# An encoder trunk step on one core: reloads of activations at the stage changes issued from POOL's queue instead of SP's

## The chip, the core and the metric

The kernel runs on one core of a Trainium2 chip, as one launch. The time is in device microseconds of that core; the smallest of the shown runs is 1948.55 us, the largest 1949.81 us. The kernel's instructions are placed by a framework that works out the waits and the order on each engine when the kernel is built: engines are PE (TensorE, matmuls), ACT (ScalarE), DVE (VectorE), POOL (GpSimd) and SP (SyncE, which here only issues DMAs).

## The reference, cut to what matters

One inference step over 512 prompt frames and 32 frames of a running stream, 544 columns in all, with a model width of 2048. There are two layers and a final norm:

```python
def rec_layer(...):                                  # layer 0
    proj = rms_norm(x, g) @ w_in
    xa, ga, xb, gb = jnp.split(proj, ...)
    ya, h_new = rg_lru(causal_conv(xa, ...), ...)    # recurrence over the frames
    yb, pool_new = pool_mix(xb, ...)                 # trailing means over 2/4/8/16 frames
    mixed = jnp.concatenate([ya * silu(ga), yb * silu(gb)], axis=-1)    # 3072 wide
    return x + mixed @ w_out, ...

def att_layer_prompt(x, g, w_in, w_out):             # layer 1
    q, k, v, gt = att_inputs(x, g, w_in)             # rms_norm(x, g) @ w_in, 16 heads of 128
    o = ...                                          # stick-breaking attention, 128-query blocks
    return x + (o * silu(gt)) @ w_out, k, v

y = rms_norm(x, norm_final)
```

All of it is in float32, and the outputs are y, k, v and the new states of the recurrent layer.

## The kernel before, in words

**Products.** Activations lie transposed, 128 features on the partitions and 544 frames along a row, so a 2048-wide activation is 16 such rows and the 3072-wide `mixed` is 24. A float32 product is made of three matmuls of a shorter type: each operand is split into a high part (a rounded copy, ACT) and the rest (a subtraction, DVE), and `mm3` (L108, L109, L110) multiplies high by high, low of x by high of w, and high of x by low of w. Weights come in pieces of 128 x 768 through `raw` (L195, on SP's queue, into seven buffers `wraw`) and are split by `wsplit` (L203 on ACT, L204 on DVE, into three pairs `wh`, `wl`); a `wraw` buffer is free when L204 has read it. PE runs without a loop, one output block after another.

**Blocks.** Twelve rows of an activation form a 2 x 2 block matrix, of two groups of six rows and two halves of 272 frames; the four quarters are called B11, B12, B21, B22. A `unit` multiplies two output blocks at once with a scheme of seven block products in place of eight; it needs the quarters and four sums and differences of them (T1 to T4) in split form. These forms lie in seven slots (`XH`, `XL`), where T4 has the slot of B12. A `plain_unit` needs only the quarters. Rows past the twelve are kept whole and split (`XP`, the names `xp`), and `rest` multiplies them.

**Stage changes.** An activation that one stage writes (`mixd`, `x2g` and `ogd` are such tensors in DRAM, as is `xgd` in the first layer) is read back, since the next stage needs it in block form. The stores go through `store` and `flush` (L326, SP's queue). The reads go through three functions, which the change touches:

- `fetch` (L233, its DMA at L237) loads one third of a quarter, two rows of 272 frames (128 x 2 x 272, 272 KB). `quarters` loads all four quarters, twelve DMAs, while the last unit of the stage before is still running, as its slots come free. `sums_by_pairs` loads quarters again for the sums T1 to T3: three DMAs for each of three pairs, then two subtractions and an addition on DVE (L283, L284, L285) and the splits (L230 on ACT, L231 on DVE); then three more loads for T4.
- `mixed_rows` (L776, its DMA at L780) loads rows 12 to 23 of `mixd`, a row of 128 x 544 (272 KB) with each DMA.
- `rows` (L1033, its DMA at L1037) loads rows 12 to 15 of `x2g` or `ogd` in the same way.

There are 92 such loads: 12 of `xgd`, in the first layer, for the sums alone, and three stage changes. The first change goes from the first layer's input product to its output product: quarters of `mixd` in the last unit, then the twelve rows, which `plain_unit` uses one after another, then the sums, 36 loads. The second goes from the first layer's output to head 0 of the second layer: quarters of `x2g` in the last unit, then four rows and the sums, 28 loads. The third goes from head 15 to the output product of the second layer: quarters of `ogd`, and much later its four rows, 16 loads.

**What sets the order.** Functions called hooks are run between the block products of a unit (the numbers in `quarters`, and the dictionaries given to `unit`); a load is written in the code one or two hooks ahead of its split. Each engine executes its own list in order, and the build's scheduler orders that list by its own estimates, so a load that stands on another queue can also move instructions of other engines. SP's list holds the weights' loads, the stores and, before the change, the 92 loads, some of them behind weight loads that wait for a `wraw` buffer. POOL's list holds a few copies, memsets and selects (for example L875 to L882, which build masks at the start of the second layer), and one DMA, the store of the last row of `mixd` (L766). A tile from the pool `tp` (`T()` in the code) takes a load's data: 8 buffers in the first layer's input product, 21 in its output product, 14 in the second layer.

**Around these.** Results leave PE's banks (`pp`, four of them) by evictions: on DVE L810 (with L809) in the first layer's output product, and L449 (with L447) in the attention's projection, where the result is also scaled by `rbc`. `L578` is a small POOL copy in the recurrent stage and `L694` a memset there.

Of the kernel before, what the change touches and what calls it, by code (L numbers as in the profile page):

```python
# [42 lines left out]
NS = 6  # L43
# [18 lines left out]
def trunk_step(ctx, tc, xT, w_in_rec, w_out_rec, gates, pool_w, vecs, st_h, st_conv, st_pool,  # L62
               w_in_att, w_out_att, ck, cv, y, kout, vout, hout, convout, poolout):
    nc = tc.nc
# [12 lines left out]
    def T(dt=F32, shape=(P, N)):  # L77
        return pools.tp.tile(list(shape), dt, tag="T", name=nm("T"))
# [146 lines left out]
    def fresh_row(j):  # L225
        XP.append(tuple(xs.tile([P, N], F32R, tag=f"xp{q}{j}", name=nm("xp")) for q in "hl"))
        return XP[-1]

    def xsplit(h, l, src):
        nc.scalar.activation(h, src, AF.Copy)  # L230
        nc.vector.tensor_tensor(l, src, f(h), ALU.subtract)  # L231

    def fetch(src, s, c):  # L233

        k, h = RAW[s]
        t = T(shape=(P, 2, HN))
        nc.sync.dma_start(t, src[:, k + 2 * c:k + 2 * c + 2, h])  # L237
        return t

    def made(s, c, t):  # L240
# [27 lines left out]
    def sums_by_pairs(src):  # L268
# [3 lines left out]
        def load(c):  # L272
            def fn():
                st[c] = [fetch(src, s, c) for s in (B12, B11, B22)]
            return fn
# [14 lines left out]
        def lastload():  # L290
            for c in range(NS // 2):
                st[c] = fetch(src, B21, c)
# [160 lines left out]
    mixd = dp.tile([P, 24, N], F32, tag="mixd", name="mixd")  # L453
    x2d = dp.tile([P, KT, N], F32, tag="x2d", name="x2d")
    x2g = dp.tile([P, KT, N], F32, tag="x2g", name="x2g")
    with ExitStack() as l0:
# [206 lines left out]
        for n in range(1, NRB):  # L663
            c = SimpleNamespace()
# [62 lines left out]
        for g4 in range(NPG):  # L727
            c = SimpleNamespace(ms=[])
# [43 lines left out]
    with ExitStack() as l0b:  # L772
# [3 lines left out]
        def mixed_rows(j0, j1):  # L776
            ts = []
            for j in range(j0, j1):
                t = T()
                nc.sync.dma_start(t, mixd[:, 2 * NS + j, :])  # L780
                ts.append(t)

            def fn():
                for j, t in zip(range(j0, j1), ts):
                    if j < 4:
                        hi, lo = fresh_row(j)
                    else:
                        hi, lo = T(F32R), T(F32R)
                        XP.append((hi, lo))
                    xsplit(hi, lo, t)  # L790
            pend.append(fn)
# [29 lines left out]
        for u in range(KT // 2):  # L821
            srcs = (w_out_rec[2 * u], w_out_rec[2 * u + 1])
            load, out = x2_out(u, SimpleNamespace())
            if u == 0:
                plain_unit(srcs, out, {
                    0: lambda: mixed_rows(0, 4),
                    1: lambda: (made_rows(), mixed_rows(4, 7)),
                    2: lambda: (made_rows(), mixed_rows(7, 10)),
                    3: lambda: (made_rows(), mixed_rows(10, 12)),
                    4: lambda: (made_rows(), load())})  # L830
            elif u == 1:
                plain_unit(srcs, out, {
                    0: loads[0],
                    1: lambda: (makes[0](), loads[1]()),
                    2: lambda: (makes[1](), loads[2]()),
                    3: lambda: makes[2](),
                    4: load, 5: lastload})
            else:
                hk = {2: load}
                if u == 2:  # L840
                    hk[0] = three
                last = u == KT // 2 - 1
                if last:
                    quarters(x2g, hk)
                unit(srcs, out, hk, LAST if last else ORDER)
# [4 lines left out]
    with ExitStack() as l1:  # L850
# [151 lines left out]
        def s_av(c):  # L1002
            w2, o_ps = c.w2, c.o
            mm3(o_ps, w2[:, 0, :P], w2[:, 1, :P], w2[:, 0, P:], w2[:, 1, P:], False, True)
            ob = e()[:, :P]
            for hh in range(4):
                rows = slice(hh * DEC, (hh + 1) * DEC)
                nc.vector.tensor_copy(ob[rows], o_ps[rows, hh * P:(hh + 1) * P])
            c.ob = ob
# [23 lines left out]
        def rows(src):  # L1033
            ts = []
            for j in range(4):
                t = T()
                nc.sync.dma_start(t, src[:, 2 * NS + j, :])  # L1037
                ts.append(t)

            def fn():  # L1040
                for j, t in enumerate(ts):
                    hi, lo = fresh_row(j)
                    xsplit(hi, lo, t)
            return fn
# [4 lines left out]
        for h in range(NH):  # L1049
            hh, G = h % 4, h // 4  # L1050
            c = SimpleNamespace()
            ha, hb = {}, {}
            if h == 0:
                rps = att_tile()
                box = []

                def spread_rbc():
                    with tc.high_priority():
                        nc.scalar.activation(rbc, rstd_spread(rps, box[0]), AF.Copy)
                with_hooks(ha, {0: [lambda: pend.append(rows(x2g))],  # L1060
                                1: [lambda: box.append(rstd_sums(rps, 0, N)), one, lambda: pend.pop()()],
                                2: [two], 3: [three],
                                4: [spread_rbc]})
            else:
                with_hooks(ha, {1: [lambda: (v_turn(prev), w_turn(prev))], 4: [lambda: av(h - 1, prev)]})
# [199 lines left out]
```

## Time and profile before

| what | value |
|---|---|
| time, median of 3 runs | 1948.99 us (1948.55 to 1949.81) |
| the profiled execution: time | 1951.53 us |
| the profiled execution: span | 1949.7 us |
| mean granted clock of TensorE | 0.994 of full speed |
| PE busy | 1908.4 us, 98% of the span |
| DVE, ACT, POOL busy | 1469.1, 915.6, 176.6 us |
| moved by DMA | 257.01 MB, 132 GB/s on the mean |
| hardware queue q1, which most DMAs use | 253.25 MB, 43.3% of the DMA engines' time |
| software queue q0 | 0.28 MB, 0.0% |
| loads of `mixd` (36): size, median from issue to landing | 272 KB, 4.8 us |

How to read it: the span reaches from the first to the last instruction, and the execution's own time lies 1.8 us above it. The clock is the share of TensorE's full speed that was granted. L12 is line 12 of the kernel; a group is written as line, engine, operation, output <- inputs. SPq stands for SP's queue of DMA issues; an issue's own duration is the time for which it holds its engine, and the landing comes later. Buffer numbers in names are left out in the profile and shown in the orders below.

### The profile page before, as it was taken

The page shows a single profiled execution, that of the slowest core. Times are in us where ns is not written, and L with a number is a line of the kernel's source. Part 1 is how long each engine was busy: PE and PEld are TensorE (multiplying, and loading weights), DVE is VectorE, ACT ScalarE, POOL GpSimd, SP SyncE. Part 2 cuts the span into 40 slices and gives each one's busy share as a digit, 9 for nine tenths or more (in the row PEclk, how much of TensorE's full clock was granted, in tenths as well). Part 3 has the DMA queues.
Part 4 walks back from the last instruction along what each step waited for, and adds up shares of the span by engine and source line. Part 5 has one row for each costly group of instructions (what it writes and reads, how often), then busy time and mean ns, then how long its engine had stood idle before and what let it go on. Part 6 is the DMA issues. An engine that isn't in the chain of part 4 may idle for free.

```text
span 1949.7 us, 37295 instructions
## 1 busy us (share of the span) xinstructions
PE 1908.4 (98%) x14962; PEld 1886.8 (97%) x14962; DVE 1469.1 (75%) x2390; ACT 915.6 (47%) x1281; POOL 176.6 (9%) x294
## 2 busy tenths in 40 slices
PE   8999999999999999999999999999999999999997
PEld 8999999999999999999999999999999999999997
DVE  8766687689888666566988888888888888864358
ACT  7666666664334443344444444444444534442233
POOL 0000012011110000000111111110111101100000
PEclk9999999999999999999999999999999999999998
DMA  6455444333336645457333333334333433365334
GB/s 220 119 147 149 118 140 122 99 98 115 104 104 211 214 145 157 134 176 230 101 100 104 112 112 109 103 114 119 94 104 115 128 97 104 112 214 172 104 101 152
DMA packets 129948, 257.01 MB, mean 132 GB/s; under 512 B 15920, under 2 KB 40752, under 8 KB 129776
## 3 DMA queue, kind: packets, MB, share of 16 engines
q1 hardware_dynamic: 128544, 253.25, 43.3%
q8 instruction: 117, 1.92, 0.4%
q10 hardware_dynamic: 1152, 1.11, 0.2%
q14 instruction: 55, 0.45, 0.1%
q0 software_dynamic: 80, 0.28, 0.0%
HBM read 217.64 MB, written 36.95 MB: 131 GB/s over the span
## 4 chain that ended last, share of the span: by engine, by line
PE 76%; DVE 12%; DMA 6%; issue 4%; ACT 2%; POOL 0%; SPq 0%; DVEq 0%; POOLq 0%; ACTq 0%
PE pp L108 23%; PE pp L110 23%; PE pp L109 23%; DVE wl L204 4%; DMA wraw<-in_w_in_att 2%; DVE big L906 1%; DMA T<-mixd 1%; DMA T<-x2g 1%; DVE xl L231 1%; PE pm L109 1%; PE pm L110 1%; PE pm L108 1%; ACT wh L203 1%; PE pa L923 1%; DVE e L447 1%
## 5 line engine op out<-in xcount | busy, mean ns | idle before, releaser
L108 PE MATMUL pp<-xh,wh 128*128 128x272 f32 x3186 | 922.4, 290 | 12.2 <-ACT wh L203 7.4
L110 PE MATMUL pp<-xh,wl 128*128 128x272 f32 x3186 | 919.2, 289 | 5.4 <-DVE wl L204 4.8
L109 PE MATMUL pp<-xl,wh 128*128 128x272 f32 x3186 | 917.7, 288 | 1.2 <-DVE xl L231 1.1
L203 ACT ACTIVATE wh<-wraw 128x768 fp32r<-128x768 f32 (+2 forms) x619 | 482.2, 782 | 804.3 <-PE pp L109 565.8
L204 DVE TENSOR_TENSOR wl<-wraw,wh 128x768 fp32r<-128x768 f32 (+2 forms) x619 | 541.4, 878 | 187.3 <-ACT wh L203 180.5
L108 PEld LDWEIGHTS pp<-xh,wh 128*128 128x128 f32 x3186 | 601.9, 189 | 14.2 <-ACT wh L203 7.6
L110 PEld LDWEIGHTS pp<-xh,wl 128*128 128x128 f32 x3186 | 601.0, 189 | 9.4 <-DVE wl L204 9.2
L109 PEld LDWEIGHTS pp<-xl,wh 128*128 128x128 f32 x3186 | 601.5, 189 | 2.3 <-DVE xl L231 1.8
L108 PE MATMUL pp<-xp,wh 128*128 128x272 f32 x1152 | 330.5, 288 | 2.0 <-ACT xp L230 2.0
L110 PE MATMUL pp<-xp,wl 128*128 128x272 f32 x1152 | 331.3, 288 | 0.0
L109 PE MATMUL pp<-xp,wh 128*128 128x272 f32 x1152 | 330.0, 287 | 0.1
L108 PEld LDWEIGHTS pp<-xp,wh 128*128 128x128 f32 x1152 | 216.9, 189 | 3.3 <-ACT xp L230 2.2
L110 PEld LDWEIGHTS pp<-xp,wl 128*128 128x128 f32 x1152 | 216.6, 188 | 0.1
L109 PEld LDWEIGHTS pp<-xp,wh 128*128 128x128 f32 x1152 | 216.2, 188 | 0.5 <-DVE xp L231 0.5
L447 DVE TENSOR_TENSOR e<-pp,e 128x272 f32<-128x272 f32 x156 | 65.7, 439 | 41.8 <-PE pp L110 38.0
L408 DVE TENSOR_TENSOR e<-pp,e 128x272 f32<-128x272 f32 x180 | 73.9, 431 | 4.8 <-PE pp L110 4.7
L109 PE MATMUL pp<-T,wh 128*128 128x272 f32 x256 | 73.2, 289 | 0.2 <-DVE T L231 0.2
L110 PE MATMUL pp<-T,wl 128*128 128x272 f32 x256 | 72.9, 287 | 0.0
L108 PE MATMUL pp<-T,wh 128*128 128x272 f32 x256 | 71.9, 289 | 0.9 <-ACT T L230 0.6
L230 ACT ACTIVATE xh<-T 128x544 fp32r<-128x544 f32 x72 | 46.6, 655 | 53.0 <-DVE T L283 15.8
L209 ACT ACTIVATE T<-T 128x544 fp32r<-128x544 f32 (+1 forms) x72 | 45.2, 645 | 42.4 <-DMA T<-in_cv 17.2
L231 DVE TENSOR_TENSOR xl<-T,xh 128x544 fp32r<-128x544 f32 x72 | 50.5, 721 | 12.4 <-ACT xh L230 12.3
(243 smaller groups left out, 2055.7 us busy)
## 6 DMA issues: line engine op xcount, KB each, us to landing
wraw<-in_w_in_att SPq DMA_DIRECT2D x128, 384.0 KB, 3.5
wraw<-in_w_in_rec SPq DMA_DIRECT2D x96, 384.0 KB, 3.5
wraw<-in_w_out_rec SPq DMA_DIRECT2D x64, 384.0 KB, 3.5
wraw<-in_w_in_att SPq DMA_DIRECT2D x64, 256.0 KB, 3.3
wraw<-in_w_in_rec SPq DMA_DIRECT2D x48, 256.0 KB, 3.4
wraw<-in_w_out_att SPq DMA_DIRECT2D x32, 384.0 KB, 4.0
T<-mixd SPq DMA_DIRECT2D x36, 272.0 KB, 4.8
wraw<-in_w_out_att SPq DMA_DIRECT2D x32, 256.0 KB, 3.3
```

The costliest lines, as they stand in the source:

```text
L108: nc.tensor.matmul(out, wh, xh, start=start, stop=False)
L109: nc.tensor.matmul(out, wh, xl, start=False, stop=False)
L110: nc.tensor.matmul(out, wl, xh, start=False, stop=stop)
L203: nc.scalar.activation(hi, src, AF.Copy)
L204: nc.vector.tensor_tensor(lo, src, f(hi), ALU.subtract)
L209: nc.scalar.activation(a, src, AF.Copy)
L230: nc.scalar.activation(h, src, AF.Copy)
L231: nc.vector.tensor_tensor(l, src, f(h), ALU.subtract)
L408: nc.vector.tensor_tensor(sm[name], acc[p], sm[other], ALU.add)
L447: nc.vector.tensor_tensor(src, bk, addend, ALU.add)
L906: nc.vector.tensor_tensor_scan(inc[:, o:o + w][:, ::-1], s, s, 1.0, ALU.mult, ALU.min)
L923: nc.tensor.transpose(wt[:, bk, cc:cc + P], be[:, o + kb * P:o + (kb + 1) * P], ident)
```

## The change

In three places a DMA is issued by `nc.gpsimd` in place of `nc.sync`, that is by POOL's queue instead of SP's. Sizes, sources, destinations and the code's order stay as they are.

```diff
@@ fetch
         t = T(shape=(P, 2, HN))
-        nc.sync.dma_start(t, src[:, k + 2 * c:k + 2 * c + 2, h])
+        nc.gpsimd.dma_start(t, src[:, k + 2 * c:k + 2 * c + 2, h])
         return t
@@ mixed_rows
                 t = T()
-                nc.sync.dma_start(t, mixd[:, 2 * NS + j, :])
+                nc.gpsimd.dma_start(t, mixd[:, 2 * NS + j, :])
                 ts.append(t)
@@ rows
                 t = T()
-                nc.sync.dma_start(t, src[:, 2 * NS + j, :])
+                nc.gpsimd.dma_start(t, src[:, 2 * NS + j, :])
                 ts.append(t)
```

SP's list goes from 806 rows to 714, POOL's from 282 to 374. Three places of the order follow; rows with a minus stand there before, rows with a plus after.

SP's list at the first stage change, where the rows of `mixd` (T) stood between loads of the output product's weights (`wraw_8290`, `8332` and `8387`):

```order
 L195 DMA wraw_8290<-in_w_out_rec 128x768
-L780 DMA T_7635<-mixd 128x544
-L780 DMA T_7637<-mixd 128x544
-L780 DMA T_7639<-mixd 128x544
-L780 DMA T_7641<-mixd 128x544
 L195 DMA wraw_8332<-in_w_out_rec 128x768
-L780 DMA T_7701<-mixd 128x544
-L780 DMA T_7703<-mixd 128x544
-L780 DMA T_7705<-mixd 128x544
-L780 DMA T_7761<-mixd 128x544
```

All twelve rows left this list; on POOL's they stand one behind the other, right behind the twelve quarter loads of `mixd` and the store L766.

POOL's list at the second stage change, where it builds masks (`m`) for the attention and where the loads of `x2g` now follow:

```order
 L880 AFFINE_SELECT m_10843<-m_10843 32x32
 L882 AFFINE_SELECT m_10844<-m_10844 32x32
+L1037 DMA T_10871<-x2g 128x544
+L1037 DMA T_10873<-x2g 128x544
+L1037 DMA T_10875<-x2g 128x544
+L1037 DMA T_10877<-x2g 128x544
+L237 DMA T_10938<-x2g 128x2x272
+L237 DMA T_10940<-x2g 128x2x272
+L237 DMA T_10942<-x2g 128x2x272
+L237 DMA T_10944<-x2g 128x2x272
```

The four rows and the loads for the sums stand behind the memsets and selects of POOL; on SP's list three weight loads stood between them.

DVE's list at the same change, in the sums of `x2g`; T_10938 to T_10954 are the loaded thirds of quarters in the order of their loads, the first three belonging to the first pair:

```order
 L285 TENSOR_TENSOR T_10940<-T_10942,T_10940 128x544
 L231 TENSOR_TENSOR xl_1549_11015<-T_10938,xh_1548_11014 128x544
+L204 TENSOR_TENSOR wl_11193<-wraw_11190,wh_11192 128x512
+L231 TENSOR_TENSOR xl_1551_11017<-T_10940,xh_1550_11016 128x544
 L283 TENSOR_TENSOR T_10948<-T_10948,T_10944 128x544
-L231 TENSOR_TENSOR xl_1551_11017<-T_10940,xh_1550_11016 128x544
+L283 TENSOR_TENSOR T_10954<-T_10954,T_10950 128x544
 L284 TENSOR_TENSOR T_10944<-T_10944,T_10946 128x544
 L231 TENSOR_TENSOR xl_1553_11019<-T_10948,xh_1552_11018 128x544
 L285 TENSOR_TENSOR T_10946<-T_10948,T_10946 128x544
+L231 TENSOR_TENSOR xl_1549_11015<-T_10944,xh_1548_11014 128x544
```

The third pair's first subtraction, which needs the ninth load (T_10954), moved up behind the second pair's, and a split of the second pair (from T_10944) moved up too; the evictions L449 of head 0 stand further down.

## What the change is forecast to do

> **What bounds the kernel now.** I read the page first, then the busy times in slices of 10 us, then PE's waits, and only then the queues.
>
> The page's busy line of PE, and the chain of work that ended last:
>
> ```profile
> PE 1908.4 (98%) x14962; PEld 1886.8 (97%) x14962; DVE 1469.1 (75%) x2390; ACT 915.6 (47%) x1281; POOL 176.6 (9%) x294
> PE 76%; DVE 12%; DMA 6%; issue 4%; ACT 2%; POOL 0%; SPq 0%; DVEq 0%; POOLq 0%; ACTq 0%
> ```
>
> PE carries the kernel: 1949.7 - 1908.4 = 41.3 us of idle is all that better feeding can win. The moved loads matter only where PE idles near them. The slices there (columns: stretch, length, busy PE, PEld, DVE, ACT and POOL with their counts, clock, DMA share, GB/s):
>
> ```profile
> 610.00:620.00 10.00, 9.83 (x79) 9.61 (x78) 8.50 (x17) 6.50 (x10) 0.00 (x0) 1.00 0.96 326
> 620.00:630.00 10.00, 9.08 (x73) 8.87 (x72) 7.23 (x10) 3.58 (x6) 0.68 (x1) 1.00 0.49 141
> 630.00:640.00 10.00, 7.63 (x55) 6.79 (x54) 4.51 (x6) 4.12 (x6) 0.00 (x0) 1.00 0.95 312
> 640.00:650.00 10.00, 9.16 (x69) 8.53 (x68) 5.98 (x8) 5.31 (x8) 0.00 (x0) 1.00 0.41 127
> 650.00:660.00 10.00, 8.34 (x65) 8.00 (x64) 4.67 (x8) 4.72 (x7) 0.00 (x0) 1.00 0.57 197
> 690.00:700.00 10.00, 9.46 (x75) 9.24 (x74) 9.82 (x15) 5.54 (x9) 0.00 (x0) 1.00 0.45 134
> 700.00:710.00 10.00, 9.11 (x73) 8.89 (x72) 8.12 (x15) 3.27 (x4) 0.00 (x0) 1.00 0.64 188
> ...
> 920.00:930.00 10.00, 6.85 (x47) 6.66 (x46) 10.00 (x17) 5.48 (x9) 0.69 (x1) 0.85 0.51 150
> 930.00:940.00 10.00, 10.00 (x68) 10.00 (x67) 9.34 (x15) 4.46 (x8) 2.78 (x1) 0.81 0.34 108
> 960.00:970.00 10.00, 9.04 (x73) 8.82 (x72) 10.00 (x15) 4.38 (x7) 1.77 (x2) 1.00 0.39 120
> ...
> 1710.00:1720.00 10.00, 8.87 (x71) 8.65 (x70) 9.59 (x15) 7.88 (x12) 2.61 (x4) 1.00 0.76 230
> 1720.00:1730.00 10.00, 8.93 (x74) 8.65 (x73) 9.33 (x18) 5.60 (x8) 0.88 (x1) 1.00 0.74 234
> ```
>
> Idle PE time is 10 minus its column. First transition (610 to 660 and 690 to 710): 0.17 + 0.92 + 2.37 + 0.84 + 1.66 + 0.54 + 0.89 = 7.4 us. Second: 3.15 at 920 to 930 and 0.96 at 960 to 970, and the clock's loss there, (0.15 + 0.19) x 10 = 3.4 us of work. Third: 1.13 + 1.07 = 2.2 us. Together 17.1 us, the whole stake. The fourth set of moved loads, of xgd in the first layer, stands at 262 to 296 us, where PE has no idle slice; I put it at 0.
>
> What ended the larger of these waits, by PE's waits (total, times, longest), of 620 to 720 and, in the last row, of 920 to 930:
>
> ```profile
> PE pp L108 <- ACT xp L230: 2.0, 1, 2.0
> PE pp L108 <- DVE T L810: 1.7, 1, 1.7
> PE pp L110 <- DVE wl L204: 1.4, 2, 0.9
> PE pp L109 <- DVE xl L231: 0.9, 1, 0.9
> ...
> PE pp L108 <- DVE T L449: 3.1, 1, 3.1
> ```
>
> Only the first and the fourth wait for a split of a moved load itself (xp of a row, xl of a quarter). L810 and L449 are evictions that free PSUM banks, and wl is a weight's split: there a load counts only through DVE, which executes in order.
>
> **The change, first transition.** The SP queue before:
>
> ```profile
> 590.89 11.32 SPq L195 DMA_DIRECT2D wraw<-in_w_out_rec  x6
> 602.26 1.45 SPq L237 DMA_DIRECT2D T<-mixd  x3
> ...
> 629.36 1.75 SPq L780 DMA_DIRECT2D T<-mixd  x4
> 633.30 0.33 SPq L195 DMA_DIRECT2D wraw<-in_w_out_rec  x1
> 633.68 3.02 SPq L780 DMA_DIRECT2D T<-mixd  x6
> 644.51 0.33 SPq L195 DMA_DIRECT2D wraw<-in_w_out_rec  x1
> 644.89 0.43 SPq L780 DMA_DIRECT2D T<-mixd  x1
> 648.09 0.33 SPq L195 DMA_DIRECT2D wraw<-in_w_out_rec  x1
> 648.47 0.43 SPq L780 DMA_DIRECT2D T<-mixd  x1
> ```
>
> The first three quarter loads stood behind six weight loads that crept out over 11.32 us, one for each weight buffer that came free. On POOL nothing stands ahead of them from 590 on. The DMA engines were then full (0.96 of 610 to 620), so what moves ahead of that stretch leaves room in it: 3 loads of 272 KB at the 326 GB/s of that slice are 3 x 0.85 = 2.6 us. The last quarter's split, for which PE waited 0.9, can come that much earlier: of 0.92 + 0.17 = 1.1 I take **-1.0** (ends: 0, if tiles rather than the queue hold them, and -1.1).
>
> The rows hang on another thing. The one store that POOL's queue carries already, and its landing:
>
> ```profile
> 626.61 0.68 POOL L766 DMA_DIRECT2D mixd<-T  x1 [36.76 <-DVE T L754]
> DMA to landing us min/median/max: 2.5/2.5/2.5
> ```
>
> It lands at 626.6 + 2.5 = 629.1 and the rows read what it writes; SP issued the first at 629.36. The wait of 2.0 on row one therefore stays but for **-0.3**. Then POOL would issue a row each 0.68: twelve from 629.1 to 636.6, where SP took until 648.47 because three weights stood between. Rows five to ten come some 1 us sooner, eleven and twelve 9 to 12. Of the 0.84 in 640 to 650 I take all: **-0.8** (ends 0 and -1.2). The 1.66 of 650 to 660 is the bank's eviction L810 behind a weight split in DVE's order: 0. Of 0.54 + 0.89, waits for wl behind a full DVE (9.82 of 10), I take a quarter, **-0.4**. First transition: -1.0 - 0.3 - 0.8 - 0.4 = **-2.5 us**; ends 0 and -1.1 - 0.3 - 1.2 - (0.54 + 0.89) = -4.0.
>
> **Second transition.** POOL must first finish its memsets and selects, which stand ahead of the loads on its queue; SP did not have to wait for them. POOL's last select, SP's first three loads, the landing of the quarter loads issued from 900 to 920, and DVE's first subtraction and first eviction:
>
> ```profile
> 906.36 0.21 POOL L882 TENSOR_SCALAR_AFFINE_SELECT m<-m 32x32 f32<-32x32 f32 x1
> ...
> 905.20 1.28 SPq L1037 DMA_DIRECT2D T<-x2g  x3
> ...
> DMA to landing us min/median/max: 5.1/5.5/9.1
> ...
> 917.60 0.72 DVE L283 TENSOR_TENSOR T<-T,T 128x544 f32<-128x544 f32 x1 [2.48 <-DMA T<-x2g]
> 927.12 0.78 DVE L449 TENSOR_TENSOR T<-pp,rbc 128x272 f32<-128x272 f32 x2
> ```
>
> POOL starts at 906.57, 1.4 later than SP, but runs through: at 0.68 each the third sum load (the seventh in all) is issued at 906.57 + 6 x 0.68 = 910.7 and the ninth (the thirteenth) at 914.7. With 5.1 they land at 915.8 and 919.8. DVE begins 917.6 - 915.8 = 1.8 sooner. But the new DVE order puts two more half-microsecond steps (0.64 from start to start) ahead of L449: 14 steps took 927.12 - 917.60 = 9.5, 16 take 10.8, so the eviction comes at 915.8 + 10.8 = 926.6, **-0.5**. One of the two needs the ninth load, at 915.8 + 5.1 = 920.9 in that row: it is there by 1.1. No two-row load from POOL is in the trace; from below 0.68 bounds it (the one-row store), from above I take twice that, for twice the rows. At 1.36 the ninth is issued at 906.57 + 4 x 0.68 + 8 x 1.36 = 920.2, lands at 925.3, and the eviction, eight steps or 5.7 on, at 931.0: +3.9. I take 0.68, since a load from SP cost 0.43 whether of one row or two. The clock's 3.4 stays (the wait shrinks to 2.6); if it goes, -3.4 more. Of the 0.96 at 960, behind a DVE that is 1.8 ahead, I take **-0.7**. Second: **-1.2**, ends +3.9 and -7.5.
>
> **Third.** DVE is at 9.59 and 9.33 of 10, so earlier loads only shift its work; nine of twelve now stand ahead of the selects of the last head on POOL, 9 x 0.68 = 6.1 us from 1701 on, done before the selects are due. I take a quarter of 2.2, **-0.6** (ends +2, at 1.36 each, and -2.2).
>
> Sum: -2.5 - 1.2 - 0.6 = -4.3 us. The profiled execution took 1951.53 (span 1949.7 and 1.8 around it), the median of the runs is 1948.99; from the median, 1948.99 - 4.3 = **1944.7 us**. SP gets rid of 92 issues of 0.43, 40 us, which is worth nothing by itself, as SP waits for buffers anyway.
>
> **Rivals.** First, the transfers were hidden or full: DMA share is 0.96 and 0.95 where the loads crowd, and each load lands about when it did. Then only tile waits and orders remain: 1949.0. Trainium skill, "DMA: Bandwidth & Descriptors", section "Issuing engines are not separate DMA queues", says the same: all DMAs run on the same 16 engines, and a second issuing engine saves only sequencer time. Against it stand the holes of 0.49, 0.41 and 0.57 between 620 and 660.
>
> Second, the second transition opens fully: the wait of 3.15 closes and the clock stays up: 1944.7 - (3.15 - 0.5) - 3.4 = 1938.7. Against it, DVE is at 10.00 through that slice.
>
> Third, slower: POOL is held by DVE while it writes descriptors. POOL's copies are:
>
> ```profile
> 270.92 5.87 POOL L578 COPY xa<-stc 128x3 f32<-128x3 f32 x1 [4.65 <-DVE ev L582]
> 270.90:276.80 5.90, 5.90 (x49) 5.90 (x49) 5.87 (x10) 3.40 (x6) 5.87 (x1) 1.00 0.93 282
> L578 POOL COPY xa<-stc x16: 208/551/7347, 33.5 to 398.9; 128x3 f32<-128x3 f32 x16
> 489.25 0.11 POOL L694 MEMSET big<- 128x15 f32 x1
> 488.00:498.00 10.00, 10.00 (x83) 10.00 (x82) 10.00 (x20) 4.32 (x6) 4.45 (x8) 1.00 0.21 58
> ```
>
> A copy of 0.55 took 5.87 while DVE ran without a pause, 5.3 us of hold. DVE is as full when the last quarters of the first transition and the last sums of the second are due. One hold at each: -4.3 + 2 x 5.3 = +6.3, 1955.3 us. It decides from holds of 4.3 in sum. Against it: a memset, which only writes, took 0.11 beside a DVE at 10.00 of 10. Trainium skill, "SBUF — State Buffer", "Who interferes with whom": a DVE instruction with two SBUF inputs blocks only GpSimd instructions that read SBUF; its box on the SWDGE trap has descriptor writing locked out only by DVE's 2-port modes. The two rows agree with the first sentence; no DMA from POOL beside a busy DVE is in this trace (L766 ran in a pause).
>
> That the change does not do what it says is out: 92 issues leave SP for POOL.
>
> **How the numbers follow.** Forecast 0.40, full or hidden 0.22, clock kept 0.14, held POOL 0.24. About 0.2%, 3.9 us, is what a measurement of this kernel can tell from no change. The forecast's own range is 1941.5 to 1948.0; 0.26 of its 0.40 lies below 1945.1. Faster: 0.26 + 0.14 = 0.40; same: 0.14 + 0.22 = 0.36; slower 0.24. The range runs from 1938.5 (the clock case) to 1955.5 (one hold at each).
>
> **What would show it.** Right: POOL issues of T<-mixd and T<-x2g near 0.7 us, both L780 groups done by 637, the first L283 near 916 and L449 near 926.5, PE idle from 630 to 650 below 2.5. Wrong: POOL issues of several us beside a full DVE; PE's wait for L449 longer than 3.1; slices from 610 to 640 unchanged with loads landing as before.

## The result, and the profile after

The changed kernel takes 1957.66 us (median of 9 runs, 1953.10 to 1960.09) where the kernel before takes 1948.61 us (9 runs, 1946.74 to 1952.44). The ratio is 1.0040, with a 95% interval of 1.0029 to 1.0051: 7.8 us slower (1948.61 x 0.0040; the two medians themselves lie 9.0 us apart), against a forecast of 4.3 us faster, and above the range. The profiled execution took 1957.66 us, its span is 1955.6. The executions of one kernel agree within 0.5%, but for one of the kernel before (10627.61 us) and one of `early_x` below (2646.37 us), which are left out of the ratios.

The busy line of the page:

```profile
PE 1912.4 (98%) x14962; PEld 1891.8 (97%) x14962; DVE 1469.1 (75%) x2390; ACT 912.9 (47%) x1281; POOL 226.6 (12%) x386
```

PE's idle time is 1955.6 - 1912.4 = 43.2 us, where before had 41.3; PE's busy time grew by 4.0, for the same 14962 matmuls. So 4.0 of the 5.9 us of lost span lie in matmuls that took longer. Where it lies, three long stretches show, one around each stage change (columns as in the slices above; the count of PE's matmuls is the second number of a pair). First of the kernel before, then of the kernel after:

```profile
600.00:750.00 150.00, 142.27 (x1111) 139.35 (x1110) 100.49 (x152) 64.03 (x92) 0.68 (x1) 1.00 0.63 196
860.00:1000.00 140.00, 134.93 (x1037) 132.83 (x1036) 112.17 (x176) 67.30 (x96) 16.79 (x28) 0.98 0.52 158
1690.00:1760.00 70.00, 67.80 (x536) 67.04 (x535) 46.55 (x72) 30.43 (x43) 6.58 (x13) 1.00 0.61 189
```

```profile
600.00:750.00 150.00, 144.43 (x1108) 142.77 (x1107) 100.94 (x153) 62.72 (x92) 22.85 (x35) 0.97 0.60 192
860.00:1000.00 140.00, 133.90 (x1024) 131.64 (x1024) 110.18 (x175) 66.88 (x96) 37.31 (x54) 0.98 0.48 151
1690.00:1760.00 70.00, 66.01 (x508) 65.20 (x507) 46.71 (x73) 29.39 (x42) 14.84 (x25) 0.98 0.58 179
```

At full pace a slice of 10 us holds 82 matmuls, 0.122 us each. The three stretches hold 3, 13 and 28 fewer: 0.4, 1.6 and 3.4 us, 5.4 of the 5.9. The first is even although PE idles less there; its clock is 0.97 instead of 1.00. Of the slices of 10 us after, those around the four stretches of lower clock, one at 870 in which PE idled, and ahead of them one in which DVE was full:

```profile
610.00:620.00 10.00, 10.00 (x82) 9.99 (x81) 10.00 (x19) 7.63 (x14) 2.02 (x3) 1.00 0.78 260
630.00:640.00 10.00, 7.59 (x43) 6.73 (x42) 5.95 (x8) 5.44 (x8) 4.59 (x9) 0.83 0.99 363
690.00:700.00 10.00, 7.21 (x46) 6.66 (x45) 7.37 (x14) 4.87 (x8) 0.72 (x1) 0.82 0.38 96
700.00:710.00 10.00, 10.00 (x70) 10.00 (x70) 8.07 (x15) 3.38 (x4) 0.00 (x0) 0.84 0.71 231
870.00:880.00 10.00, 8.73 (x68) 8.29 (x67) 7.20 (x13) 4.18 (x7) 1.45 (x2) 1.00 0.65 215
900.00:910.00 10.00, 6.68 (x48) 6.46 (x47) 5.96 (x10) 4.89 (x7) 2.42 (x7) 0.90 0.55 164
910.00:920.00 10.00, 10.00 (x65) 10.00 (x65) 5.21 (x15) 3.64 (x7) 9.76 (x19) 0.76 0.81 260
1720.00:1730.00 10.00, 7.54 (x61) 7.22 (x60) 10.00 (x17) 4.59 (x7) 0.55 (x1) 1.00 0.60 187
1730.00:1740.00 10.00, 10.00 (x71) 10.00 (x70) 7.38 (x12) 3.11 (x4) 1.13 (x6) 0.83 0.51 167
```

Four waits are each followed by a lower clock: 1.7 + (1.8 + 1.6) + (1.0 + 2.4) + 1.7 = 10.2 us of full pace, by (1 - clock) x 10, where before's one such stretch near a stage change cost 3.4. That is an upper end, since part of such a slice is idle. The trace's clock record stands at 0.50 of full speed in these stretches ("half clock"), for 3.41 or 6.83 us at a time; 3.41 us in a slice of 10 give the 0.83. In return the small waits of before at 610 to 630 and at 640 to 660 are gone. What ended the four waits, by PE's waits of 600 to 660, 685 to 705, 900 to 950 and 1705 to 1735:

```profile
PE pp L108 <- ACT xp L230: 2.2, 1, 2.2
...
PE pp L108 <- ACT wh L203: 2.0, 1, 2.0
...
PE pa L137 <- DVE sqacc L123: 3.3, 1, 3.3
...
PE pm L913 <- DVE T L449: 2.5, 1, 2.5
```

The kernel before has no wait of the second kind there, and of the last two kinds it has these (900 to 950 and 1705 to 1735):

```profile
PE pa L137 <- DVE sqacc L123: 0.3, 1, 0.3
...
PE pm L913 <- DVE T L449: 1.1, 1, 1.1
```

Two of the four stand at places that the prediction didn't price: ACT's split of a weight at 694 (it had only DVE's there) and `sqacc`, the sum of squares for the norm, at 904. At the first change the queue of POOL did what was forecast of it. At the second it began its loads at 911.84 where 906.57 was forecast: its memsets wait for `sqacc` too (13.41 us), so what delays that sum delays them. POOL's issues at the first and the second change, in POOL's timeline (start, length, engine and line):

```profile
628.20 4.78 POOL L780 DMA_DIRECT2D T<-mixd  x9 [2.44 <-DMA mixd<-T]
635.94 0.54 POOL L780 DMA_DIRECT2D T<-mixd  x1 [0.19 <-issue]
...
907.47 0.98 POOL L875 MEMSET qp<- 128x512 f32 x2 [13.41 <-DVE sqacc L123]
911.84 2.17 POOL L1037 DMA_DIRECT2D T<-x2g  x4
```

And all 24 loads of quarters and sums of mixd, by their source line (shortest, median and longest issue in ns):

```profile
L237 POOL DMA_DIRECT2D T<-mixd x24: 712/722/729, 590.3 to 690.1; - x24
```

A row costs 0.54 and a load of two rows 0.72 to issue, and no issue was stretched, not even in the slice 610 to 620, where DVE was at 10.00. What did go wrong is seen at 694, in DVE's and ACT's lists:

```profile
693.34 0.73 DVE L299 TENSOR_TENSOR T<-T,xh 128x544 f32<-128x544 f32 x1 [2.63 <-DMA T<-mixd]
...
694.73 0.66 ACT L230 ACTIVATE xh<-T 128x544 fp32r<-128x544 f32 x1 [5.47 <-DVE T L299]
695.29 0.83 ACT L203 ACTIVATE wh<-wraw 128x768 fp32r<-128x768 f32 x1
```

DVE waits 2.63 for the last load of T4's sums, ACT 5.47 for what DVE makes of it, and the split of a weight (L203), which needs none of this, stands behind on ACT's list. PE has by then run ahead, and waits for the weight. The split itself is no later than in the kernel before, where it stands at 695.61; but in `mixd_rows` below, whose sums are loaded by SP and whose PE is ahead as well, it stands at 693.61. The last load of the sums was issued at 686.77 there. In the changed kernel POOL issued it at 690.15, having waited for a split on DVE:

```profile
690.15 0.72 POOL L237 DMA_DIRECT2D T<-mixd  x1 [6.01 <-DVE xl L231]
```

So what had been gained ahead of 694 did not reach the last load of the sums.

### The profile page after: what moved, and what is told of

The parts are those of the page before. It is cut to its first block, busy times and chain, and to the rows that moved or that the text cites. A ratio compares the mean times of both kernels' runs of the same rounds, so it can differ in the third digit from the quotient of the medians.

```text
span 1955.6 us, 37392 instructions
## 1 busy us (share of the span) xinstructions
PE 1912.4 (98%) x14962; PEld 1891.8 (97%) x14962; DVE 1469.1 (75%) x2390; ACT 912.9 (47%) x1281; POOL 226.6 (12%) x386
## 4 chain that ended last, share of the span: by engine, by line
PE 77%; DVE 10%; DMA 6%; issue 4%; ACT 1%; POOL 1%; DVEq 0%; SPq 0%; POOLq 0%; ACTq 0%
PE pp L110 23%; PE pp L108 23%; PE pp L109 23%; DVE wl L204 3%; DMA wraw<-in_w_in_att 2%; DVE big L906 1%; DMA T<-mixd 1%; PE pa L923 1%; DMA T<-x2g 1%; PE pm L109 1%; DMA wraw<-in_w_in_rec 1%; PE pm L110 1%; PE pm L108 1%; DVE xl L231 1%; ACT wh L203 1%
## 5 line engine op out<-in xcount | busy, mean ns | idle before, releaser
L203 ACT ACTIVATE wh<-wraw 128x768 fp32r<-128x768 f32 (+2 forms) x619 | 482.0, 782 | 819.8 <-PE pp L109 574.2
L108 PEld LDWEIGHTS pp<-xh,wh 128*128 128x128 f32 x3186 | 604.6, 190 | 13.0 <-ACT wh L203 10.2
L231 DVE TENSOR_TENSOR xl<-T,xh 128x544 fp32r<-128x544 f32 x72 | 50.2, 722 | 13.8 <-ACT xh L230 13.8
```

The costliest lines, as they stand in the source:

```text
L108: nc.tensor.matmul(out, wh, xh, start=start, stop=False)
L203: nc.scalar.activation(hi, src, AF.Copy)
```

## Experiments

My theory after this result: **late loads in front of other work.** DVE and ACT execute in order, and their lists hold instructions that wait for a reload ahead of weight splits and evictions. SP's one queue had spaced the reloads between the weights in the order of need; on POOL each starts as soon as its tile is free, so that some land later for the instruction that needs them first. The rivals: the loss is the clock's alone (waits no longer in sum, but in larger pieces), or it comes from POOL's own place in the second change, behind the selects, or from a slower start of each load on POOL. The last has against it the landings in the changed kernel's own profile: the quarters of mixd took 5.1 us from issue to landing before and 4.6 after, those of x2g 4.7 and 4.3 (medians).

Each time below is a median of 5 to 12 executions, each ratio is to the kernel before. Rows that begin with "PE p" are PE's waits: for whom, total us, count, longest.

**One activation at a time.** `fetch` and `rows` choose the queue by the tensor that they read; the others stay on SP (in `mixd_only`, `mixed_rows` is on POOL too).

```diff
-        nc.sync.dma_start(t, src[:, k + 2 * c:k + 2 * c + 2, h])
+        (nc.gpsimd if src is moved[0] else nc.sync).dma_start(t, src[:, k + 2 * c:k + 2 * c + 2, h])
```

> Only the loads of mixd (36) are issued by POOL, the other 56 by SP as before. Theory clock: the loss comes from single PE waits that pass about 2.3 us and are followed by some 5 us at half clock; at the first stage change the waits themselves shrink by about 2 us (7.7 to 5.6) and two half-clock stretches cost 1.8 and 2.6, so the time is 0 to 3 us above before, ratio 1.000 to 1.0015, with half-clock stretches after a wait near 630 and one near 694. Theory queues: POOL's loads and SP's weight loads share the DMA engines and both land later; this change has the most loads that crowd (36 of 92), so about 36/92 of the 7.8 us, 3 us, and the sum of PE's waits between 600 and 710 above that of before, with no need for a clock drop.

> Only the loads of x2g (28) are issued by POOL. Theory clock: between 860 and 960 the waits change little in sum, and one half-clock stretch takes the place of another, so 1 to 2 us above before (ratio 1.0005 to 1.001), the wait for sqacc at the start of head 0 being the longest. Theory queues: 28/92 of 7.8, 2.4 us, from later landings of quarters and weights.

> Only the loads of ogd (16) are issued by POOL. Both theories expect a loss here: the second ogd load lands late and DVE, which has no slack there, idles about 2.4 us for it. Theory clock: the wait before the transposes L913 grows from 1.2 to about 2.6 and half clock follows it; 3 us above before, ratio 1.0015, of which some 1.4 is the clock. Theory queues: 16/92 of 7.8, 1.4 us, all of it waits.

Measured: `mixd_only` 1948.13 us, 1.0001 (0.9992 to 1.0010); `x2g_only` 1951.29, 1.0016 (1.0007 to 1.0025); `ogd_only` 1951.91, 1.0019 (1.0010 to 1.0028). The three add up to +0.2 + 3.1 + 3.7 = 7.0 of the 7.8 us; the rest is within the intervals. The loads of xgd were not tried alone; from 250 to 310, where they stand, PE has 481 matmuls and 60.00 busy us in the profiles of both kernels. Mixd has the most loads and loses least, which speaks against a price per load. Its profile has the wait at 694 again:

```profile
PE pp L108 <- ACT wh L203: 3.2, 1, 3.2
PE pp L108 <- ACT xp L230: 3.0, 1, 3.0
```

So what the first change gains it gives back there. By the starts of the same matmuls in the two profiles, `mixd_only` gains 3.1 us on the kernel before from 620 to 660 and loses 4.0 from 690 to 710; the changed kernel gains 3.3 and loses 4.0. In `ogd_only` the wait for L449 (2.5) is that of the changed kernel, but no half clock followed it in the profiled execution; the clock's share is taken up below.

**The second change in two parts.** Only the quarters of x2g (`quarters(x2g, hk, nc.gpsimd)`), or only its rows and sums (`sums(x2g, nc.gpsimd)`, `rows(x2g, nc.gpsimd)`), on POOL:

```diff
-    def fetch(src, s, c):
+    def fetch(src, s, c, queue=nc.sync):
...
-        nc.sync.dma_start(t, src[:, k + 2 * c:k + 2 * c + 2, h])
+        queue.dma_start(t, src[:, k + 2 * c:k + 2 * c + 2, h])
```

> The kernel before, with only the 12 quarter loads of x2g (in the last unit of the first layer, 837 to 893 us) issued by POOL; PE's order is that of before, DVE's differs in ten rows. Theory order: the loss of the x2g loads is made here, where PE had no wait before: DVE's list now has additions and splits that wait for a load ahead of weight splits and evictions, so waits of 1.6 at 877 and 3.5 at 903 appear, the second with half clock behind it; ratio 1.001 to 1.002, all of x2g_only's. Theory queue at the second change itself: the quarters are harmless and the loss comes from rows and sums that stand behind POOL's selects; ratio 1.000.

> The kernel before, with only the four rows and the 12 loads for the sums of x2g issued by POOL (905 to 922 us), that is the part that I costed at -1.2 us with ends of +3.9 and -7.5. Theory order: no loss, ratio 0.9990 to 1.0003, the first eviction L449 0.5 to 1 us earlier than before. Theory queue at the second change itself: ratio 1.001 to 1.002.

Measured: `x2g_quarters` 1953.88 us, 1.0024 (1.0015 to 1.0034); `x2g_sums` 1945.53 us, 0.9990 (0.9981 to 0.9998). This part of the study is clear: the rows and sums, which I had costed, gain 1.9 us, and the quarters, which I had not, lose 4.7. The loads began as worked out, but the eviction did not come earlier for it; POOL's and DVE's rows in `x2g_sums`:

```profile
907.12 2.17 POOL L1037 DMA_DIRECT2D T<-x2g  x4
...
915.82 0.73 DVE L283 TENSOR_TENSOR T<-T,T 128x544 f32<-128x544 f32 x1 [0.39 <-DMA T<-x2g]
...
927.80 0.78 DVE L449 TENSOR_TENSOR T<-pp,rbc 128x272 f32<-128x272 f32 x2
```

DVE begins at 915.82 where I had 915.8. L449 comes at 927.80, later than the 927.12 of before and not at 926.6: DVE waited once more, 1.10 us at 922.24 for the ninth load, which took 7.2 us to land where I had given it 5.1. By the starts of the same matmuls in the two profiles, `x2g_sums` gains 0.2 us on the kernel before from 900 to 930, where L449 is, and 1.6 from 930 to 980. In `x2g_quarters` DVE is held at two places, for xT and for a late quarter; first its timeline, then PE's wait behind it:

```profile
875.45 0.44 DVE L809 TENSOR_TENSOR T<-T,e 128x272 f32<-128x272 f32 x1 [2.25 <-DMA T<-in_xT]
...
897.08 0.73 DVE L231 TENSOR_TENSOR xl<-T,xh 128x544 fp32r<-128x544 f32 x1 [2.31 <-ACT xh L230]
897.72 0.43 DVE L810 TENSOR_TENSOR T<-T,pp 128x272 f32<-128x272 f32 x1
```

```profile
PE pa L137 <- DVE sqacc L123: 3.8, 1, 3.8
```

L809 waits 2.25 for a load that SP issues, because the build's order now has it ahead of the preparation of a weight; L231 waits 2.31 for a quarter, and the eviction L810 stands right behind it. From there the delay goes on to the sum of squares, for which PE waits 3.8, against 0.3 in the kernel before and at most 1.3 in the profiles with no change there.

**Order or queue?** Only nine of the quarters on POOL (`x2g_q_b22sp`), or only the other three (`x2g_q_b22pool`):

```diff
-                    quarters(x2g, hk)
+                    quarters(x2g, hk, lambda s: nc.sync if s == B22 else nc.gpsimd)
```

> As x2g_quarters, with the last quarter's three loads (B22) back on SP; the lists of PE, DVE and ACT are word for word those of x2g_quarters, so only the queue of these three loads differs. Theory order: the split of B22's second load stands ahead of the evictions on DVE in both, so the wait of 3.5 to 4 before the sum of squares stays and the ratio too, 1.0015 to 1.0025. Theory queue: that wait comes from B22 being late on POOL; it goes, and the ratio falls to 1.001 or less.

> The reverse: only the three loads of B22 on POOL, nine on SP; the lists of PE and DVE are those of before but for one addition to sqacc. Theory order: no loss, 0.9995 to 1.0005. Theory queue: the wait at the sum of squares is there, 1.0015 or more.

Measured: `x2g_q_b22sp` 1951.06 us, 1.0013 (1.0004 to 1.0022); `x2g_q_b22pool` 1951.14 us, 1.0017 (1.0008 to 1.0025). Neither theory has it alone. PE's wait for the sum of squares, first in `x2g_q_b22sp`, then in `x2g_q_b22pool`:

```profile
PE pa L137 <- DVE sqacc L123: 1.7, 1, 1.7
```

```profile
PE pa L137 <- DVE sqacc L123: 3.2, 1, 3.2
```

With the order of `x2g_quarters` word for word, moving three loads back to SP cuts that wait from 3.8 to 1.7: the queue's part. It is not all gain, as PE then waits 1.4 for L449 instead; all its waits of 860 to 950 come to 6.4 and 6.2 us (3.8 before). Those three loads alone on POOL, with DVE's old order but for one split that changed places with an addition to `sqacc`, make a wait of 3.2. Here the late load can be seen, in ACT's timeline:

```profile
892.89 0.66 ACT L230 ACTIVATE xh<-T 128x544 fp32r<-128x544 f32 x1 [3.62 <-DMA T<-x2g]
```

The first load of B22, issued at 887.8 by POOL, lands after 5.1 us; by SP, at 887.9 in the kernel before, it landed after 3.1. What is left in `x2g_q_b22sp`, the wait at 877 behind L809 (PE busy 8.65 of 10 from 870 to 880, and 10.00 in `x2g_q_b22pool`), is the order's part. I tried to take that part away with a kernel in which the last unit's loads of xT are called a hook earlier (`hk = {1 if u == KT // 2 - 1 else 2: load}`), all on SP, and then with the nine quarters on POOL:

> Control for the next one: the kernel before with the two loads of xT of the last unit (L802) called one hook earlier, all loads on SP. In x2g_quarters and x2g_q_b22sp an addition L809, which waits for the second of them, stands ahead of a weight's preparation L400 on DVE and costs a wait of 1.6 us at 877. Here nothing is on POOL: 0.9995 to 1.0005.

> early_x with the first nine quarter loads of x2g on POOL (the last three on SP); DVE's list is that of early_x but for one split. Theory order: without L809 waiting for xT the wait at 877 goes, and what is left of x2g_q_b22sp's 2.5 us is 1 us or less: ratio 1.0005 or less, and within 0.0005 of early_x. Theory queue: the nine loads still land later, 1.0010 or more.

Measured: `early_x` 1949.36 us, 1.0009 (0.9999 to 1.0018); `b22sp_early_x` 1950.70 us, 1.0016 (1.0007 to 1.0025). The control missed its expectation, and the two differ by less than either interval. The wait at 877 is gone in both (PE busy 10.00 from 870 to 880), but both have a long wait for the sum of squares. That of `early_x`:

```profile
PE pa L137 <- DVE sqacc L123: 3.1, 1, 3.1
```

It is as long as in `x2g_q_b22pool`, with no load on another queue. So order alone can make that wait, and its length by itself does not tell the queue from the order; how the 4.7 us divide between the two stays open.

**The third change.** Only the loads of ogd, with the first three on SP (`ogd_first_sp`); with POOL's seventh to ninth load held back until the third has landed (`ogd_paced`: POOL copies an element of the tile onto itself); and with the first three on SP and the next ones held back (`ogd_both`).

```diff
-                quarters(ogd, hb)
+                quarters(ogd, hb, lambda s: nc.sync if s == B11 else nc.gpsimd)
```

> The kernel before, with 13 of the 16 loads of ogd issued by POOL; the first three (quarter B11), which are needed first, stay on SP. Theory late first loads: ogd_only loses because its second and third load are issued 1 us later and land 2.4 us later in the midst of SP's weight loads, and DVE idles for them; with them back on SP the wait before L916/L913 is that of before (1.2) and the ratio 1.000. Rival, sharing: all of POOL's ogd loads go beside the weights, whichever is first, and the loss stays, ratio 1.0015 or more.

> As ogd_only, with the lists of PE, DVE, ACT and SP word for word the same; POOL copies one element of the third, sixth and ninth loaded tile onto itself, so that its seventh to ninth load are issued only when the third has landed, and so on. The result is unchanged. Theory sharing: ogd_only loses because nine loads run at once beside SP's weights, so that the ones needed first land late; paced as SP's queue paced them, the second and third land earlier, the wait before the transposes shrinks from 2.75 towards 1.4, and the ratio falls from 1.0019 to 1.0008 or less. Rival, issue: POOL's slower start of a load is what costs; the ratio stays at 1.0015 or more.

> As ogd_first_sp (the first three loads of ogd on SP, the rest on POOL; the lists of PE, DVE, ACT and SP word for word the same), with one element of the third loaded tile copied by POOL ahead of its own loads, so that these begin when the third has landed. The copied element is overwritten by the load. Theory crowding: ogd_first_sp lost because POOL's six loads were begun within 4 us of the first and the third load landed 11 us after its issue; with them held back the third lands within 6, DVE does not idle 4.6 us for it, and PE's wait of 4.2 at 1713 is gone: ratio 1.0005 or less. Rival: holding POOL back makes its own loads late, and DVE idles for those; ratio 1.0015 or more.

Measured: `ogd_first_sp` 1953.53 us, 1.0020 (1.0011 to 1.0029); `ogd_paced` 1950.78, 1.0018 (1.0009 to 1.0027); `ogd_both` 1953.90, 1.0035 (1.0021 to 1.0048). All three missed: the loss stayed or grew. What they show is how it moves. First the split of the second load of ogd in ACT's timeline of the changed kernel, then of the kernel before:

```profile
1711.16 0.66 ACT L230 ACTIVATE xh<-T 128x544 fp32r<-128x544 f32 x1 [2.84 <-DMA T<-ogd]
```

```profile
1707.53 0.64 ACT L230 ACTIVATE xh<-T 128x544 fp32r<-128x544 f32 x1
```

The first splits stand at 1707.67 and 1706.23, so the second comes 3.5 us behind the first instead of 1.3: one of the loads needed first lands later. In `ogd_first_sp`, the landing of the seven loads issued from 1700 to 1704 (three on SP, four on POOL), the split of the third in ACT's timeline, and PE's wait:

```profile
DMA to landing us min/median/max: 4.7/8.2/11.0
```

```profile
1713.56 0.66 ACT L230 ACTIVATE xh<-T 128x544 fp32r<-128x544 f32 x1 [6.07 <-DMA T<-ogd]
```

```profile
PE pp L108 <- ACT wh L203: 3.9, 1, 3.9
```

The 11.0 is the third load on SP: five of POOL's loads, begun beside it and needed later, landed before it, and ACT stood still for 6.07. The Trainium skill, "DMA: Bandwidth & Descriptors", section "Queues, rings and completion order", says that each DMA engine takes packets in turn from the queues that have work; the trace agrees, as far as this load on SP took 11.0 us beside POOL's where it took 5.7 without them. In `ogd_both` the first three land in time, and the hold-up is further on, in ACT's timeline and in PE's waits:

```profile
1704.00 0.66 ACT L230 ACTIVATE xh<-T 128x544 fp32r<-128x544 f32 x1 [0.59 <-DMA T<-ogd]
...
1718.28 0.66 ACT L230 ACTIVATE xh<-T 128x544 fp32r<-128x544 f32 x1 [2.20 <-DMA T<-ogd]
1718.84 0.83 ACT L203 ACTIVATE wh<-wraw 128x768 fp32r<-128x768 f32 x1
```

```profile
PE pm L916 <- DVE T L452: 5.5, 1, 5.5
```

ACT waits only 0.59 for the third load, but the quarter B21, now behind the selects and in a bunch of six, lands at 1718; the weight's split again stands behind it, DVE waits 3.36 for that split ahead of its evictions, and PE waits 5.5 (L916 and L452 are L913 and L449 with the lines added). In the profile of `ogd_paced` PE's wait for L452 did shrink, to 1.4, as expected of it; but that execution (1948.47 us) was 2.3 us below the median, and the ratio did not move. In `ogd_first_sp` the crowding of the first loads is seen; that a better spacing on POOL would bring the time of before is not shown, as I found none.

**The clock.** Two kernels fill the wait for the first row of mixd with 21 matmuls that add products with zero, so that PE does not idle: `fill` on the changed kernel (with 14 more before the sum of squares), and later `before_fill` on the kernel before.

```diff
+            for _ in range(fill if m == 0 else 0):
+                nc.tensor.matmul(accs[0], XH[B11][:, 0, :P], zer[:, 0:1].to_broadcast([P, HN]), start=False, stop=False)
```

> The changed kernel with PE given work in two of the waits that precede half clock: 21 matmuls that add products with zero before the first row of mixd, and 14 that add zeros before the sum of squares in head 0. They change no result. Theory clock: the half-clock stretches at 632 and at 909 vanish (1.8 and 2.6 us), while the instructions that end the two waits come when they came: 4 us below the changed kernel, ratio to before 1.002 in place of 1.004. Theory queues: the clock is a side show, the fillers bring nothing or cost their own 2 to 5 us: ratio 1.004 or more.

> The kernel before with 21 matmuls that add products with zero ahead of the first row of mixd, loads all on SP. best_fill was 4.8 us below best where I expected 1.7, and its profile still has half clock at 635. Theory clock: the fillers take the place of the wait of 2.25 and no half clock follows in most executions: 1 to 2 us below before, 0.9990 to 0.9995. If the 4.8 us are a property of the fillers: 0.9975. Rival: the gain of best_fill came from its other orders, and here it is 1.000.

Measured: `fill` 1957.98 us, 1.0050 (1.0036 to 1.0064), no gain; `before_fill` 1943.63 us, 0.9981 (0.9973 to 0.9990), 3.7 us. The slice 630 to 640 of `ogd_only`, whose code is that of before here (the profile of before itself, 55 matmuls at a clock of 1.00, caught no half clock), and of `before_fill`:

```profile
630.00:640.00 10.00, 8.00 (x49) 7.57 (x49) 4.18 (x6) 4.12 (x6) 0.00 (x0) 0.83 0.90 292
```

```profile
630.00:640.00 10.00, 8.81 (x67) 8.18 (x67) 5.48 (x8) 5.34 (x8) 0.00 (x0) 1.00 0.91 322
```

The clock stays at 1.00 over the filled wait, and in `fill` it did so too; there, however, PE had a new wait of 7.3 us right behind the sum of squares and its fillers, put down to ACT's split of a row of x2g, for which ACT itself waited 7.67, and the whole gained nothing. In `before_fill` 21 of the 67 matmuls are fillers, so the slice holds 46 of the kernel's own, no more than the 49. By the starts of the same matmuls its profile has gained 1.5 us on before from 620 to 660, and loses 3.0 from 690 to 710, where it waits 2.7 for a weight's split and half clock follows:

```profile
700.00:710.00 10.00, 7.31 (x46) 7.09 (x45) 6.43 (x11) 2.70 (x4) 0.00 (x0) 0.83 0.44 126
```

So the profile does not show that the 3.7 us come from the filled wait.

How much of the loss is the clock's can be estimated from the executions themselves, each of which lists its mean granted clock. Over the changed kernel's nine the mean is 0.9920; over the sets of executions of the kernel before, 0.9947 to 0.9952. For `mixd_only`, `x2g_only` and `ogd_only` it is 0.9935, 0.9939 and 0.9944, beside 0.9947. The difference times the span is 5 to 6 us of the changed kernel's 7.8, and 2.3, 1.6 and 0.6 us of the parts' 0.2, 3.1 and 3.7; an upper end, since a low clock costs nothing while PE idles. So the clock is most of the whole loss but not all of it: in the first change it takes back what shorter waits gain, and in the third nearly all is waits. The same estimate gives 1.4 of the 3.7 us of `before_fill` (0.9957 against 0.9950).

**A version from the parts that gained.** The rows of mixd alone, then these with the rows and sums of x2g, then with the fillers:

```diff
-                nc.sync.dma_start(t, mixd[:, 2 * NS + j, :])
+                nc.gpsimd.dma_start(t, mixd[:, 2 * NS + j, :])
...
-        one, two, three = sums(x2g)
+        one, two, three = sums(x2g, nc.gpsimd)
```

> The kernel before, with only the 12 rows of mixd issued by POOL. By my prediction's terms this is -0.3 -0.8, -1.1 us. Theory order: mixd_only gains 2 to 3 us up to 656 and gives it back at 694, where ACT waits for the split of T4's late third load; the rows alone keep the gain, ratio 0.9985 to 0.9995. Rival: the gain up to 656 comes from the quarters of mixd, and the rows bring nothing, 1.000.

> The kernel before with only those loads on POOL that gained by themselves: the rows of mixd, and the rows and sums of x2g. If the gains of x2g_sums (0.9990) and mixd_rows (0.9995) add up: 0.9985, 1945.6 where before has 1948.5. Rival: an earlier first stage change only moves the wait to the next one, and it stays at 0.9990 to 0.9995.

> As best, with 21 matmuls that add products with zero while PE waits for the first row of mixd (a wait of 2.2 to 3.2 us, in most profiles followed by half clock at 633 to 638, worth 1.6 to 1.9 us). Theory clock: no half clock follows, 1.7 us below best, 0.9976 where best has 0.9985. Rival: half clock depends on something else, or the fillers last longer than the wait; same as best or up to 2 us above.

Measured: `mixd_rows` 1947.60 us, 0.9995 (0.9987 to 1.0004); `best` 1946.17 us, 0.9992 (0.9983 to 1.0000); `best_fill` 1941.40 us, 0.9971 (0.9959 to 0.9983). `best` is no better than `x2g_sums`, and the gain of `mixd_rows` is within its interval of zero; that the two add up to 0.9985 is neither shown nor excluded. In the profile of `mixd_rows`, whose sums are on SP, the gain of 620 to 660 is 2.3 us by the starts of the same matmuls, and only 0.3 is lost from 690 to 710, against 4.0 with the sums on POOL. The fillers are worth 4 us here as on the kernel before (0.9971 / 0.9992 = 0.9979), though half clock still followed the row's wait in the profile of `best_fill`: the gain is measured twice, its cause is not shown. `best_fill` is faster than both kernels, by 5.7 us than the one before.

## Why the prediction was wrong

PE around the quarter loads of x2g, in the kernel before:

```profile
860.00:900.00 40.00, 40.00 (x322) 40.00 (x321) 26.98 (x41) 19.96 (x30) 0.00 (x0) 1.00 0.71 219
```

- **What bounds the kernel: the step that failed.** "The moved loads matter only where PE idles near them." PE had no idle time from 860 to 900 in the kernel before, so the 12 quarter loads of x2g got no term. They cost 4.7 us (`x2g_quarters`), more than any term of my sum. PE's idle time bounds what a change can win. It says nothing of what it can lose: a busy PE is fed by lists with little slack, and an instruction that comes late makes a wait where none was. The same holds for the last load of the sums of mixd.
- **First change, -2.5 forecast, +0.2 measured** (0.9992 to 1.0010). The rows came as worked out: issued from 628.20 to 635.94 (629.1 to 636.6 forecast), with `mixd_rows` at -1.0 us, near the -0.3 and -0.8 of the terms but within its interval of zero. I followed the rows and quarters and not the last load of the sums, which POOL issued at 690.15 (686.77 in `mixd_rows`, by SP). The weight's split behind it stayed where it was in the kernel before, and PE, ahead by then, waited 2.0 us for it, with two slices of lower clock.
- **Second change, -1.2 forecast, +3.1 measured.** The costed part has the right sign and nearly the size, -1.9 measured, and DVE's start within 0.1 us. Its term for the eviction did not happen: L449 came 0.7 later than before, not 0.5 sooner, since I gave each load the shortest landing of the row 5.1/5.5/9.1, and the ninth took 7.2. What was gained lies behind it, near the 0.96 at 960 of which I took 0.7, so part of the agreement is luck. The rest is the missing term above.
- **Third change, -0.6 forecast, +3.7 measured.** "Earlier loads only shift its work" took it that loads leaving SP come earlier. Issued by the bunch, the second load was split 3.5 us behind the first instead of 1.3. With DVE at 9.59 of 10 there was little room to catch up.
- **The clock.** I took its loss as fixed (3.4) or gone, and gave no chance to its growing. Half clock followed larger single waits at more places, up to 10.2 us in the profiled execution; by the mean clocks of all executions the changed kernel loses 5 to 6 us more to it than the kernel before.
- **The rivals.** "Held POOL" gave the upper end of the range and the time nearest to the result (1955.3), by a mechanism that did not happen: the longest issue of these 24 loads was 0.729 us. That all transfers are hidden or full was wrong in the same way as the forecast. The rival that was missing is a load that lands late in front of other work; DVE's order rows showed L231 and L283 moving ahead of evictions, and I priced their busy time and one load that they wait for (the ninth, taken to be there 1.1 us early), not the others.

## What to carry to other kernels

A queue that issues loads in order also spaces them and ranks them by need; with some moved to a second queue, here, loads needed later landed before one needed first. Price such a move by the lists of the in-order engines: for each instruction that waits for a moved load, what stands behind it, and how much slack that has, also where the bounding engine does not idle today. And try the parts alone: here 16 of the 92 loads gained, and the rest hid it.

## What the runs showed of the hardware

- Half clock after short waits. In twelve profiles with the loads of mixd as before (before itself, and those of x2g, ogd and xT alone), PE's wait for the first row was about 2 us (2.0 in before); the slice 630 to 640 shows a clock of 0.83 in nine of them and 1.00 in three. The Trainium skill, "TensorE: Matmul & The Clock Gate", section "Why this matters for your kernels", warns of idle gaps above about 3 us. Here half clock followed 2 us in most executions, though not in all, so the length of the wait alone (1.8 to 2.2 in the nine, 1.9 to 2.0 in the three) does not decide it.
- A load on POOL costs its engine 0.54 us for a tile of 128 x 544 and 0.72 for one of 128 x 2 x 272, beside an idle or a full DVE; on SP one of either shape cost 0.42 to 0.44 in the median.
